# Plain fp32 products in place of three fp32r products of splits, in two transformer blocks with experts

## The chip, the cores and the metric

One core of a Trainium2 chip runs one program. Its engines work side by side, each through its own list of instructions in order, and wait for one another by semaphores: TensorE (PE; its weight loads are listed as PEld), VectorE (DVE), ScalarE (ACT), GpSimd (POOL) and SyncE (SP), whose queue issues nearly all transfers between HBM and the on-chip memory. The metric is the device time of one execution in microseconds, as the median of several runs. The profile shows one further execution.

## The reference

Two blocks run one after the other on 256 positions of width 1024, in fp32. The excerpt is cut to the products.

```python
# first block
u = rms_norm(h, attn_norm_g)
(dq, dk, dv, nq, kc, vc, ks, vs, kw, vw, ngate, mgate) = split(u @ w_in)
y_a = rms_norm(differential_attention(dq, dk, dv, lam), diff_subln_g) * (1 - lam_init)
y_b = g0 * o_c + g1 * o_s + g2 * o_w            # compressed, selected, windowed attention
h = h + (sigmoid(mg0) * (y_a @ w_branch_a) + sigmoid(mg1) * (y_b @ w_branch_b)) @ w_out
u = rms_norm(h, ffn_norm_g)
h = h + (silu(u @ w_gate) * (u @ w_up)) @ w_down
x = rms_norm(h, final_norm_g)
# second block
q, k, v, a, g = split(rms_norm(x, norm1_g) @ w_in_2)
conv = silu(layer_norm(depthwise_conv(a * sigmoid(g)) + conv_b))
x = x + concat(rms_norm(attn, attn_out_g), rms_norm(conv, conv_out_g)) @ w_out_2
h = rms_norm(x, norm2_g)
aff = softmax(h @ w_router)                      # each of 16 experts takes its 32 best positions
hid = silu(xs @ w_gate_2) * (xs @ w_up_2)        # 1024 -> 2048, per expert
out = rms_norm(x + scatter(gates * (hid @ w_down_2)), final_g)
```

## The kernel before

The 256 positions are two row blocks, t = 0 and t = 1, of 128. A wide linear layer is made in blocks of 512 output columns: `linear_steps` (L311) takes a slot with 2 MB of weights (eight pieces of 128 input rows by 512 columns), and the transposed activations `xt[t]`, and adds eight products per row block into one accumulator bank (tag `mm`, two banks).

Each of these products is made in three parts. `split` (L279) makes of a landed weight piece `wh`, a copy rounded to fp32r (ScalarE, L288), and `wl`, the rest (VectorE, L289). With a gain per row it does this in two halves through `put_hl` (L342; ScalarE L350, VectorE L351). Activations are split in the same way when they are copied out of the bank in which they were transposed. `mm3` (L297) then adds `xh·wh`, `xh·wl` and `xl·wh`. All matmuls of the first stage are recorded by the helper `MM` (L250), all transposes by `TP` (L255), so these lines stand for many places; the names of the tiles tell them apart: `mm` is a bank of a wide product, `dn` those of the feed forward's last layer, `tr` a bank for transposes, `sc` scores.

The order of TensorE's list is the order in which the code records it (`manual_schedule`). That order comes from `weave` (L234): several generators (compression, two flows of attention units, the mixer with the projections) yield the time after which they want to go on, on a clock `clock[0]` that `MM` moves on by an estimate of each product (512 columns: 0.213 us for fp32r, 0.853 for plain fp32). Work that waits for another engine is put in a list by `later(after, f)` and recorded by `flush` when the clock has passed.

The stages are: first block (nine blocks of `w_a`, one of `w_vg`, attention, `w_ab`, `w_o`); feed forward (`feed`, eleven blocks b of `w_gu` with 512 columns, 256 of gate and 256 of up, each followed by the layer down of block b - 1; `hid` is made by VectorE at L875 and transposed); second block (`w_b`, convolution, attention, `w_o2` in two halves with the activations `mixc` and `mixa`); router; 16 experts of 24 MB.

Expert weights are always plain fp32. `stream` hands out their slots by a list `turns` of twelve turns with 2 MB each; three turns are filled ahead, during the feed forward (`AH`). `ringd` (six half slots) takes the space of the split pieces after the first stage. The program on TensorE uses a slot's two 1 MB halves and so gives them back, and the next transfer of that turn is asked for on SyncE's queue.

Of the kernel before, what the change touches and what calls it, by code (L numbers as in the profile page):

```python
# [137 lines left out]
AH = [2, 7, 8]  # L138
ORDERS = [(0, 0, 0, 1, 0, 1, 1, 1), (0, 0, 0, 0, 1, 1, 1, 1), (0, 0, 1, 0, 0, 1, 1, 1), (0, 0, 0, 1, 1, 0, 1, 1), (0, 0, 1, 0, 1, 0, 1, 1), (0, 1, 0, 0, 1, 0, 1, 1)]
TURNS = [0, 4, 0, 0, 2, 0, 0, 0, 0, 0, 0, 0, 0, 0, 0, 0, 0, 0, 0, 0, 0, 0, 0, 0, 0, 0, 0, 0]  # L140

# [4 lines left out]
def _program(nc, tc, A, dbg=None):  # L146
# [9 lines left out]
    hres = es.enter_context(tc.tile_pool(name="hres", bufs=1, side="right"))  # L156
    t1 = ExitStack()
    sp = t1.enter_context(tc.tile_pool(name="sp", bufs=4))
    low = t1.enter_context(tc.tile_pool(name="low", bufs=4))
# [4 lines left out]
    low0 = [at1.enter_context(tc.tile_pool(name="low0", bufs=1))]  # L164
    spare = [at1.enter_context(tc.tile_pool(name="spare", bufs=1))]
# [40 lines left out]
    def slot_tile(pool=None):  # L206
        if pool is None:
            loads[0] += 1
            pool = ring0[0] if ring0 and loads[0] % 3 == 0 else ring
        return pool.tile([128, 4096], FT, tag="slot", name="slot")  # L210
# [38 lines left out]
    def MM(out, lhsT, rhs, start, stop):  # L249
        T.matmul(out, lhsT=lhsT, rhs=rhs, start=start, stop=stop)  # L250
        n, m = math.prod(rhs.shape[1:]), math.prod(lhsT.shape[1:])
        clock[0] += max(n, 128) * (1 if rhs.dtype == FR else 4) / 2400 * min(m, 128) / 128
# [23 lines left out]
    settings = iter(TURNS)  # L276
    splits, NX = [0], [1, 1]

    def split(src, n, gcol=None, fine=False):  # L279

        splits[0] += 1
        h = (spare[0] if spare and splits[0] % (4 + NX[0]) < NX[0] else sp).tile([128, n], FR, tag="wh", name="wh", padded_shape=[128, 1024])
        l = (low0[0] if low0 and splits[0] % (4 + NX[1]) < NX[1] else low).tile([128, n], FR, tag="wl", name="wl", padded_shape=[128, 1024])
        if fine:
            for c in (slice(0, n // 2), slice(n // 2, n)):
                put_hl(h[:, c], l[:, c], src[:, c])
        elif gcol is None:
            S.activation(h, src, AF.Copy)  # L288
            V.tensor_tensor(l, src, h.bitcast(FT), op=OP.subtract)  # L289
        else:  # L290
            w = n // 2
            for j in range(2):
                c = slice(j * w, (j + 1) * w)
                put_hl(h[:, c], l[:, c], src[:, c], col=gcol[:, j:j + 1])
        return h, l

    def mm3(out, xh, xl, wh, wl, start, stop):  # L297
        MM(out, xh, wh, start, False)
        MM(out, xh, wl, False, False)
        MM(out, xl, wh, False, stop)  # L300

# [9 lines left out]
    def linear_steps(slot, xt, evac, n=512, gcol=None, mid=None, ks=range(8), turn=None, fine=False):  # L311

        us = sorted({k // 2 for k in ks})
        turn = turn or ORDERS[next(settings)]
        hl = {j: split(slot[:, (j - us[0]) * 2 * n:(j - us[0] + 1) * 2 * n], 2 * n, None if gcol is None else gcol[:, 2 * j:2 * j + 2], fine and j < 2) for j in us}
        ps, at = [None] * 2, [0, 0]
        for t in turn:
# [5 lines left out]
            u = us[at[t]]  # L323
            at[t] += 1
            for k in (2 * u, 2 * u + 1):
                h, l = hl[u]
                c = slice((k % 2) * n, (k % 2 + 1) * n)
                mm3(ps[t][:, :n], xt[t][0][:, k], xt[t][1][:, k], h[:, c], l[:, c], k == ks[0], k == ks[-1])
            if at[t] == len(us):
                if mid is not None and t == 0:  # L330
                    mid()
                with tc.high_priority(1000):
                    evac(t, ps[t] if n == 512 else ps[t][:, :n])
# [3 lines left out]
    def linear(*args, **kw):  # L337
        for _ in linear_steps(*args, turn=(0, 0, 0, 0, 1, 1, 1, 1), **kw):
            pass
        flush()  # L340

    def put_hl(h, l, ps, scale=None, col=None):  # L342
        if scale is None and col is None:
            S.activation(h, ps, AF.Copy)
            V.tensor_tensor(l, ps, h.bitcast(FT), op=OP.subtract)
        elif col is None:
            S.activation(h, ps, AF.Copy, scale=scale)
            V.scalar_tensor_tensor(l, ps, scale, h.bitcast(FT), op0=OP.mult, op1=OP.subtract)
        else:
            S.activation(h, ps, AF.Identity, scale=col)  # L350
            V.scalar_tensor_tensor(l, ps, col, h.bitcast(FT), op0=OP.mult, op1=OP.subtract)  # L351

    def x_tiles(t):
        return [xtp.tile([128, 8, 128], FR, tag=f"xt{a}{t}", name="xt") for a in "hl"]

    def transposed(src, xt, c, scale=None, gain=None, tmp=None, high=False):

        ps = bank("tr")
        for j in range(4):
            TP(ps[:, j * 128:(j + 1) * 128], src[:, (4 * c + j) * 128:(4 * c + j + 1) * 128])  # L360
        h, l = (flat(z[:, 4 * c:4 * c + 4]) for z in xt)
        if gain is None:
            with tc.high_priority(1000 if high else 0):
                put_hl(h, l, ps, scale)
        else:
            gx = tmp()
            V.tensor_tensor(gx.rearrange("p (a b) -> p a b", a=4), ps.rearrange("p (a b) -> p a b", a=4),
                            gain[:, 4 * c:4 * c + 4, None].to_broadcast([128, 4, 128]), op=OP.mult)
            S.activation(h, gx, AF.Copy)
            V.tensor_tensor(l, gx, h.bitcast(FT), op=OP.subtract)  # L370
# [18 lines left out]
    def begin(t):  # L389
        for c in range(2):  # L390
            transposed(x0[:, t], xt[t], c, gain=attn_g, tmp=lambda: tp.tile([128, 512], FT, tag="ropeo", name="gx"))
# [225 lines left out]
    def nsa_unit(t, b, half):  # L617
# [34 lines left out]
        if todo["yb", t] == 0:  # L652
            ybT[t] = h_, l_ = [ap_.tile([128, 512], FR, tag=tag, name="ybT", padded_shape=[128, 528])
                               for tag in (("blk0", "blk1") if t == 0 else ("ybh1", "ybl1"))]
            put_hl(h_, l_, yb[t])
            mark(f"yb_done{t}", 3.3)

    def diff_unit(t, hp):
# [50 lines left out]
        if t == 0:  # L709
            todo["yah"] = ap_.tile([128, 2, 512], FR, tag="nqT", name="yah")  # L710
        yaT[t] = h_, l_ = todo["yah"][:, t], ap_.tile([128, 512], FR, tag=f"kT{t}", name="yal")
        put_hl(h_, l_, pt, col=sub8)
# [14 lines left out]

    mg = mgp.tile([128, 2, 4, 512], FT, tag="mg", name="mg")
# [8 lines left out]
    def mixer():  # L737
        W = lambda i: load(flat(A["w_a"][i]))
        yield from linear_steps(first, xt, ev_a, fine=True, turn=ORDERS[1][:1] + (begin1,) + ORDERS[1][1:])
# [4 lines left out]
        yield from linear_steps(W(4), xt, ev_dv)  # L744
        for n in range(4):
# [4 lines left out]
        for n in range(2):  # L750
            hl = [[split(wab[j][:, n * 2048 + u * 1024:n * 2048 + (u + 1) * 1024], 1024) for u in range(2)] for j in range(2)]
# [167 lines left out]
    steps = []  # L919
# [510 lines left out]
```

## Time and profile before

| | |
|---|---|
| median of 3 runs | 1444.31 us (1443.38 to 1444.76) |
| the profiled execution's own time | 1444.65 us |
| its span, first to last instruction | 1442.8 us |
| TensorE busy | 1110.6 us, 6451 matmuls |
| VectorE busy | 428.2 us |
| ScalarE busy | 322.7 us |
| transferred | 498.16 MB, mean 345 GB/s |
| granted clock of TensorE, mean | 0.897 of 2.4 GHz |

An engine's busy time is the time in which at least one of its instructions is recorded as running. Matmuls are pipelined, so one that lasts 0.39 us can be followed by the next after 0.23; what a product costs in a row of products is read from start to start. A line "x4" merges four instructions, from the first one's start to the last one's end. The chain of waits goes back from the last instruction, at each step to what released it.

### The profile page before, as it was taken

To read this page: it belongs to the slowest core of one execution; us is meant where nothing else is said; L and a number is where in the kernel's file an instruction comes from. 1 tells how busy PE (TensorE), PEld (TensorE's weight loads), DVE (VectorE), ACT (ScalarE), POOL (GpSimd) and SP (SyncE) were. 2 spreads that over 40 slices of the span, in tenths; PEclk is the share of its full clock that TensorE was granted. 3 is DMA by queue.
4 is the path that set the end of the run, shared out by engine and by line. 5 is a ranking of instruction groups with operands and counts; after the bars stand their busy time and mean duration, and the time that the engine had idled before them with its cause. 6 is when DMAs were issued, how large, how long until landed. Compare 5 with 4: busy or idle time off the path is not lost.

```text
span 1442.8 us, 15497 instructions
## 1 busy us (share of the span) xinstructions
PE 1110.6 (77%) x6451; PEld 557.9 (39%) x6451; DVE 428.2 (30%) x826; ACT 322.7 (22%) x583; POOL 33.5 (2%) x43
## 2 busy tenths in 40 slices
PE   7999999999999989766665665676666676666565
PEld 5777877888877773111211111121111121111112
DVE  6587675555562751101100100001000010010002
ACT  5466545555463630000000000000000000000001
POOL 1010000000000000000000000000000000000001
PEclk9999999999999999798998878788877897788889
DMA  8623247757546788999999999999999999999996
GB/s 313 260 92 124 100 186 284 278 219 269 176 168 191 291 339 366 427 429 431 428 429 429 429 431 427 429 431 429 429 426 429 431 427 430 428 430 430 427 429 290
DMA packets 52165, 498.16 MB, mean 345 GB/s; under 512 B 6016, under 2 KB 9088, under 8 KB 12160
## 3 DMA queue, kind: packets, MB, share of 16 engines
q1 hardware_dynamic: 52096, 497.18, 83.6%
q8 instruction: 51, 0.84, 0.2%
q14 instruction: 18, 0.15, 0.0%
HBM read 495.52 MB, written 1.64 MB: 345 GB/s over the span
## 4 chain that ended last, share of the span: by engine, by line
DMA 61%; PE 32%; DVE 4%; ACT 2%; issue 1%; SPq 0%; POOLq 0%; POOL 0%; ACTq 0%; DVEq 0%
DMA half<-in_e_d 21%; PE mm L250 21%; DMA half<-in_e_u 20%; DMA slot<-in_e_u 6%; DMA slot<-in_e_g 6%; PE dn L250 4%; PE sc L250 2%; DMA half<-in_e_g 2%; DMA slot<-in_e_dl 2%; DMA slot<-in_e_d 2%; PE tr L255 2%; PE mm L1305 2%; DVE wl L289 1%; DMA slot<-in_w_a 1%; DMA half<-in_e_dl 1%
## 5 line engine op out<-in xcount | busy, mean ns | idle before, releaser
L1305 PE MATMUL mm<-slot,xg 128*32 128x512 f32 x1536 | 240.1, 757 | 151.1 <-DMA slot<-in_e_u 96.3
L250 PE MATMUL mm<-wh,xt 128*128 128x512 f32 (+1 forms) x896 | 291.1, 395 | 2.8 <-DVE ropeb L446 1.8
L250 PEld LDWEIGHTS mm<-wh,xt 128*128 128x128 f32 x896 | 168.1, 189 | 41.6 <-issue 5.1
L1336 DVE TENSOR_TENSOR x<-acc,x 128x512 f32<-128x512 f32 x60 | 41.5, 691 | 462.1 <-PE acc L1334 462.1
L250 PE MATMUL mm<-wl,xt 128*128 128x512 f32 (+1 forms) x448 | 174.4, 389 | 0.7 <-DVE wl L289 0.4
L1329 PE MATMUL sc<-half,hT 128*32 128x512 f32 x720 | 122.1, 764 | 64.3 <-DMA half<-in_e_d 64.2
L1305 PEld LDWEIGHTS mm<-slot,xg 128*32 128x32 f32 x1536 | 47.7, 125 | 319.3 <-issue 119.9
L289 DVE TENSOR_TENSOR wl<-slot,wh 128x1024 fp32r<-128x1024 f32 (+1 forms) x104 | 124.6, 1211 | 73.5 <-ACT wh L288 72.8
L288 ACT ACTIVATE wh<-slot 128x1024 fp32r<-128x1024 f32 (+1 forms) x104 | 106.9, 1042 | 66.6 <-PE mm L250 49.8
L1312 DVE TENSOR_TENSOR sil<-sil,mm 128x512 f32<-128x512 f32 x16 | 11.0, 687 | 293.3 <-PE mm L1305 293.3
L1334 PE MATMUL acc<-eo,owT 128*128 128x512 f32 x120 | 78.1, 737 | 21.8 <-DVE x L1336 11.8
L250 PEld LDWEIGHTS mm<-wl,xt 128*128 128x128 f32 x448 | 84.6, 189 | 17.9 <-DVE wl L289 1.7
L1305 PE MATMUL mm<-half,xg 128*32 128x512 f32 x512 | 74.2, 666 | 20.2 <-DMA half<-in_e_u 11.0
L1350 ACT ACTIVATE eo<-sc 128x512 f32<-128x512 f32 x15 | 9.0, 597 | 357.2 <-PE sc L1329 357.2
L1329 PEld LDWEIGHTS sc<-half,hT 128*32 128x32 f32 x720 | 17.9, 123 | 163.2 <-DMA half<-in_e_d 142.7
L351 DVE SCALAR_TENSOR_TENSOR wl<-slot,pr,wh 128x512 fp32r<-128x512 f32 x88 | 62.8, 765 | 41.4 <-ACT wh L350 41.4
L1325 ACT ACTIVATE owT<-tr 128x256 f32<-128x256 f32 x16 | 6.1, 383 | 299.1 <-PE tr L1323 299.1
L350 ACT ACTIVATE wh<-slot,pr 128x512 fp32r<-128x512 f32 x88 | 58.1, 715 | 46.9 <-PE mm L250 31.2
L1329 PE MATMUL sc<-slot,hT 128*32 128x512 f32 x240 | 39.7, 791 | 26.6 <-DMA slot<-in_e_d 26.1
L1334 PEld LDWEIGHTS acc<-eo,owT 128*128 128x128 f32 x120 | 20.6, 216 | 89.5 <-DVE x L1336 33.5
L1311 ACT ACTIVATE sil<-mm 128x512 f32<-128x512 f32 x16 | 9.6, 597 | 192.4 <-PE mm L1305 192.4
L1305 PEld LDWEIGHTS mm<-half,xg 128*32 128x32 f32 x512 | 13.4, 119 | 72.2 <-DMA half<-in_e_u 41.3
(330 smaller groups left out, 972.4 us busy)
## 6 DMA issues: line engine op xcount, KB each, us to landing
slot<-in_e_g SPq DMA_DIRECT2D x48, 2048.0 KB, 24.4
slot<-in_e_u SPq DMA_DIRECT2D x48, 2048.0 KB, 29.2
half<-in_e_d SPq DMA_DIRECT2D x90, 1024.0 KB, 24.4
half<-in_e_g SPq DMA_DIRECT2D x32, 1024.0 KB, 29.2
half<-in_e_u SPq DMA_DIRECT2D x32, 1024.0 KB, 31.6
slot<-in_e_d SPq DMA_DIRECT2D x15, 2048.0 KB, 29.2
slot<-in_w_gu SPq DMA_DIRECT2D x11, 2048.0 KB, 8.1
slot<-in_w_a SPq DMA_DIRECT2D x7, 2048.0 KB, 8.7
```

Source lines behind the costliest of these rows:

```text
L250: T.matmul(out, lhsT=lhsT, rhs=rhs, start=start, stop=stop)
L255: T.transpose(out, src, ident if idn is None else idn)
L288: S.activation(h, src, AF.Copy)
L289: V.tensor_tensor(l, src, h.bitcast(FT), op=OP.subtract)
L350: S.activation(h, ps, AF.Identity, scale=col)
L351: V.scalar_tensor_tensor(l, ps, col, h.bitcast(FT), op0=OP.mult, op1=OP.subtract)
L1305: T.matmul(ps[32 * j:32 * j + 32], lhsT=xg[:, k, s0:s0 + 32], rhs=slot[kk][:, j * 512:(j + 1) * 512], start=k == 0, stop=k == 7)
L1311: S.activation(sil, gu[0], AF.Silu)
L1312: V.tensor_tensor(sil, sil, gu[1], op=OP.mult)
L1329: T.matmul(ps[32 * j:32 * j + 32, :c.stop - c.start], lhsT=hT2[:, q * 128 + 32 * j:q * 128 + 32 * j + 32], rhs=slot[n][:, j * 512 + c.star ...
L1334: T.matmul(ps, lhsT=owT[:, t * 128:(t + 1) * 128], rhs=eo, start=True, stop=True)
L1336: V.tensor_tensor(x[:, t, k], ps, x[:, t, k], op=OP.add)
```

## The change

All products named above are made once, in plain fp32, with the landed weights as moving operand. `split`, `mm3`, `put_hl` and the pools of the split pieces are gone; activations are copied out of the transpose bank once (`out_of`, in turn by ScalarE and VectorE, or VectorE with the gain). The gain of the feed forward's norm goes from the weights to the activations. In the space of the split pieces stands `ringl`, two full slots that serve for all loads and later for experts; `ringd` keeps two of six half slots. `linear_steps` has one default order, t = 0 and then t = 1, and in the feed forward a `flush` before each of the two. The clock counts every product at two columns per tick. The convolution's weights `w_cv` are loaded early in the first block.

```diff
-AH = [2, 7, 8]
-ORDERS = [(0, 0, 0, 1, 0, 1, 1, 1), ...]
+AH = [2, 5, 8]
...
+    ringl = es.enter_context(tc.tile_pool(name="ringl", bufs=2))
-    sp = t1.enter_context(tc.tile_pool(name="sp", bufs=4))
-    low = t1.enter_context(tc.tile_pool(name="low", bufs=4))
...
-        clock[0] += max(n, 128) * (1 if rhs.dtype == FR else 4) / 2400 * min(m, 128) / 128
+        clock[0] += max(n, 128) * 2 / 2400 * min(m, 128) / 128 * lhsT.shape[0] / 128
...
-    def mm3(out, xh, xl, wh, wl, start, stop):
-        MM(out, xh, wh, start, False)
-        MM(out, xh, wl, False, False)
-        MM(out, xl, wh, False, stop)
...
-    def linear_steps(slot, xt, evac, n=512, gcol=None, mid=None, ks=range(8), turn=None, fine=False):
+    def linear_steps(slot, xt, evac, n=512, ks=8, turn=(0, 0, 0, 0, 1, 1, 1, 1)):
...
-            for k in (2 * u, 2 * u + 1):
-                h, l = hl[u]
-                c = slice((k % 2) * n, (k % 2 + 1) * n)
-                mm3(ps[t][:, :n], xt[t][0][:, k], xt[t][1][:, k], h[:, c], l[:, c], k == ks[0], k == ks[-1])
+            for k in (at[t], at[t] + 1):
+                MM(ps[t][:, :n], xt[t][:, k], slot[:, k * n:(k + 1) * n], k == 0, k == ks - 1)
...
+    def out_of(dst, ps, scale=None):
+
+        turns_of[0] += 1
+        if turns_of[0] % 2:
+            S.activation(dst, ps, AF.Copy, scale=1.0 if scale is None else scale)
+        elif scale is None:
+            V.tensor_copy(dst, ps)
...
+        w_cv.append(load(flat(A["w_cv"]), pool=ringx))
...
-            yield from linear_steps(slot, xt, ev, gcol=pp("ffn_g"), turn=(flush, 0, 0, 0, 0, flush, 1, 1, 1, 1) if b == 0 else None)
+            yield from linear_steps(slot, xt, ev, turn=(flush, 0, 0, 0, 0, flush, 1, 1, 1, 1))
...
-    turns += [[ringc[0]], [ringc[1]], [ring], ringc[3:1:-1], [ring], [ringd[4], ringd[0]], [ringd[2], ringd[1]], [ringd[3], ringd[5]]]
+    turns += [[ringl], [ringc[0]], [ringc[1]], [ring], ringc[3:1:-1], [ring], ringd, [ringl]]
```

Two places show how TensorE's list moves. The first is a block of the feed forward. Before, the list of TensorE at the end of a block's 48 products (both row blocks, in three parts each):

```order
L250 MATMUL mm<-wh,xt 128x512 x2
L250 MATMUL mm<-wl,xt 128x512
L250 MATMUL mm<-wh,xt 128x512
L255 MATMUL tr<-fst,hid 128x128 x2
L250 MATMUL dn<-wh,hh 128x512
L250 MATMUL dn<-wl,hh 128x512
L250 MATMUL dn<-wh,hl 128x512
```

The same place in the changed kernel, one whole block (`slot` is the landed weights):

```order
L245 MATMUL mm<-slot,xt 128x512 x8
L250 MATMUL tr<-fst,hid 128x128 x2
L245 MATMUL mm<-slot,xt 128x512 x8
L245 MATMUL dn<-slot,hh 128x512 x8
L250 MATMUL tr<-fst,hid 128x128 x2
```

The transposes of t = 0 stood behind the products of both row blocks and now stand between them, right behind the products of t = 0 from which `hid` is made.

The second place is the end of the first attention: the difference units of t = 0 and t = 1 (`dkT`, `dqT` are their keys and queries, `a` the difference of the two softmaxes, `ya` its product with V, `yn` the normed result). Before, TensorE's list between the ya of t = 0 and the next step holds projections of the gate blocks:

```order
L250 MATMUL mm<-wl,xt 128x512
L250 MATMUL mm<-wh,xt 128x512
L250 MATMUL ya<-dv_1016,pt 128x128 x2
L250 MATMUL mm<-wh,xt 128x512
L250 MATMUL mm<-wl,xt 128x512
L250 MATMUL mm<-wh,xt 128x512 x2
```

The same place in the changed kernel, from the scores of the second unit of t = 0 on:

```order
L245 MATMUL sc<-dkT,dqT 128x128 x4
L250 MATMUL tr<-fst,a_963 128x128 x2
L245 MATMUL ya<-dv_580,pt 128x128 x2
L245 MATMUL sc<-dkT,dqT 128x256 x4
L250 MATMUL tr<-fst,a_1010 128x128 x2
L245 MATMUL ya<-dv_580,pt 128x128 x2
L250 MATMUL tr<-fst,a_1042 128x128 x4
L250 MATMUL tr<-fst,yn 128x128 x4
L245 MATMUL sc<-dkT,dqT 128x256 x4
L245 MATMUL mm<-slot,yaT 128x512 x4
```

The projections of the gates now all stand ahead of this place; between the steps of the units nothing wide is left.

## Rows read from the trace of the kernel before

**Rows 1.** The page's chain that ended last, shares of the span by engine.

```profile
DMA 61%; PE 32%; DVE 4%; ACT 2%; issue 1%; SPq 0%; POOLq 0%; POOL 0%; ACTq 0%; DVEq 0%
```

**Rows 2.** Windows: from:to, us, engines' busy us (instructions), clock, DMA share, GB/s.

```profile
0.00:212.00 212.00, 201.11 (x1176) 157.71 (x1177) 147.91 (x330) 117.81 (x227) 19.23 (x20) 1.00 0.49 183
212.00:376.00 164.00, 162.48 (x735) 133.27 (x734) 94.28 (x134) 88.30 (x134) 0.57 (x2) 1.00 0.64 244
376.00:545.50 169.50, 160.42 (x1016) 126.26 (x1018) 94.02 (x190) 84.09 (x150) 7.31 (x12) 0.97 0.64 238
```

**Rows 3.** A window among the experts, same columns (PE, PEld, DVE, ACT, POOL).

```profile
900.00:1100.00 200.00, 132.59 (x729) 29.82 (x722) 19.76 (x35) 5.33 (x10) 0.00 (x0) 0.80 1.01 429
```

**Rows 4.** Timeline at the seam: start, us, engine, line, operation, out<-in.

```profile
529.15 0.39 PE L250 MATMUL mm<-wh,mixa 128*128 128x512 f32 x1
...
529.58 1.28 SPq L805 DMA_DIRECT2D half<-in_e_d  x3
...
545.55 1.19 SPq L805 DMA_DIRECT2D half<-in_e_g  x2
```

**Rows 5.** The window just before the first freed slot.

```profile
540.00:545.00 5.00, 4.17 (x25) 2.93 (x28) 1.94 (x6) 0.52 (x1) 0.00 (x0) 0.69 0.43 179
```

**Rows 6.** TensorE's groups by form: tiles, count, busy us, mean ns, idle before.

```profile
L250 PE MATMUL mm<-wl,xt 128*128 128x512 f32 x432 | 169.7, 393 | 0.7 <-DVE wl L289 0.4 <-DVE sub L437 0.2
...
L250 PE MATMUL dn<-wl,hh 128*128 128x512 f32 x88 | 34.3, 390 | 0.0
...
L250 PE MATMUL mm<-wl,mixa 128*128 128x512 f32 x16 | 7.0, 434 | 0.0
...
L250 PE MATMUL mm<-wl,xt 128*128 128x280 f32 x16 | 4.7, 292 | 0.0
```

**Rows 7.** The chain of waits in the feed forward: start, us, what.

```profile
264.08 10.89 PE mm L250 x48
...
275.19 4.13 PE dn L250 x18
...
280.93 10.90 PE mm L250 x48
```

**Rows 8.** Plain products: timeline, and last the durations min/median/max of L1366.

```profile
550.29 8.79 PE L1305 MATMUL mm<-slot,xg 128*32 128x512 f32 x80
558.90 3.62 PE L1305 MATMUL mm<-half,xg 128*32 128x512 f32 x32
...
575.18 1.12 PE L1334 MATMUL acc<-eo,owT 128*128 128x512 f32 x2
576.24 1.06 PE L1305 MATMUL mm<-slot,xg 128*32 128x512 f32 x8
...
1420.23 1.13 PE L1366 MATMUL mm<-eo,owT 128*128 128x256 f32 x4 [0.50 <-ACT eo L1399]
...
L1366 PE MATMUL mm<-eo,owT x12: 275/379/483, 1420.2 to 1435.2; 128*128 128x256 f32 x8, 128*128 128x128 f32 x4
```

**Rows 9.** The page's group of VectorE's subtractions, busy us, mean ns.

```profile
L289 DVE TENSOR_TENSOR wl<-slot,wh 128x1024 fp32r<-128x1024 f32 (+1 forms) x104 | 124.6, 1211 | 73.5 <-ACT wh L288 72.8
```

**Rows 10.** Timeline of TensorE at the feed forward's first block; in brackets idle before.

```profile
222.64 0.39 PE L250 MATMUL mm<-wh,xt 128*128 128x512 f32 x1
224.17 0.44 PE L255 MATMUL tr<-fst,hid 128*128 128x128 f32 x2 [1.15 <-DVE hid L875]
```

**Rows 11.** Timeline of the difference units: scores, difference `a`, square, `yn`.

```profile
129.10 0.71 PE L250 MATMUL sc<-dkT,dqT 64*128 64x128 f32 x8
...
133.76 0.61 DVE L678 SCALAR_TENSOR_TENSOR a<-e,dsm 128x128 f32<-128x128 f32 x2
...
166.19 0.58 ACT L697 ACTIVATE yq<-ya 128x512 f32<-128x512 f32 x1
...
170.25 0.69 DVE L702 TENSOR_TENSOR yn<-ya,rsa 128x512 f32<-128x512 f32 x1
```

**Rows 12.** A window behind three short waits of the second attention.

```profile
515.00:520.00 5.00, 5.00 (x17) 3.96 (x16) 2.48 (x7) 0.63 (x2) 0.54 (x1) 0.70 1.02 429
```

## What the change should do to the time: the prediction

> **What bounds the kernel now.** I read the chain of waits first [rows 1]: 61% of the span hangs on landing transfers, 32% on TensorE, 4% on VectorE, 2% on ScalarE. Those shares mix two stages, so I cut the span. From 0 to 545.5 us [rows 2] TensorE shows 201.11, 162.48 and 160.42 us of work in stretches of 212, 164 and 169.5 us: 524.0 of 545.5, with transfers at 0.49 to 0.64 of their capacity. VectorE is at 336 us there, ScalarE at 290. So the first stage, both blocks and the feed forward, is bound by TensorE, and its idle time is only 21.5 us in all. The second stage, the experts, is bound by HBM: between 900 and 1100 us the engines of the transfers are full at 429 GB/s while TensorE idles a third of the time [rows 3].
>
> The seam decides how the first stage reaches the end. Expert weights run through 24 half slots of 1 MB. The last of these is asked for in a burst that begins at 529.58 us, and the next expert transfer after that burst starts at 545.55 us, when the first expert product has given a slot back [rows 4]. Between 540 and 545 us the transfer engines are only 0.43 busy [rows 5]: everything that fits has landed, and the stream waits for the first free slot. From there on it is saturated. So the end lies 1442.8 - 545.55 = 897.2 us after the first freed slot, and a delay of TensorE before it should move the end by the same amount.
>
> **The change, part by part.** *Products.* What goes: 600 groups of three fp32r products [rows 6]: 432 + 88 + 16 + 16 with "wl" as moving operand, and three more kinds of 16 like the mixa row (ybT, yah, mixc). Sixteen are 280 columns wide; by width that is 584 + 16 x 280/512 = 592.75 groups of 512. One fp32r product takes 10.89 us / 48 = 0.227 us from start to start, and a full period of the feed forward (72 products, 4 transposes) takes 280.93 - 264.08 = 16.85 us [rows 7]. A group costs 3 x 0.227 = 0.681 us.
>
> What comes in its place is one plain fp32 product, which the trace of before shows only in other shapes [rows 8]. Each plain product is recorded as two matmuls: the scatter's two per product. Eighty records of the experts' quarter-array products, four side by side, take 558.90 - 550.29 = 8.61 us, so 0.4305 us per set of four at 512 columns. The full-array product of 256 columns in the last expert gives four records (two products) in 1.13 us; the last lasts 0.379, the first 0.483 since it waits 0.104 for its own weights, so the steps are (1.13 - 0.379 - 0.104) / 3 = 0.216 us per record, with the loads of the later ones hidden. Twice the width makes at most 0.431. Both say 2 x 0.431 = 0.862 us per product of 512. The dear end is the scatter itself, 576.24 - 575.18 = 1.06 us, which stands alone between products of another shape. In the changed kernel the products stand in unbroken rows of 4 to 16, like the first two. I take 0.862; 0.861 is the low end, and 0.88 (a tenth of the way to 1.06) is where I end the range.
>
> So TensorE's own work grows: 592.75 x (0.862 - 0.681) = +107 us (+107 to +118).
>
> The Trainium skill has a rule against this change. "TensorE: Matmul & The Clock Gate", section "Part 3: Packing small matmuls — row/col tiling", says that a weight load runs under products in flight only if it is for another row group. All rows of the array are used here, so by that rule each of the two records would pay its load. The steps of 0.216 and 0.227 us in the trace contradict it, both with full-height weights. The sum by the rule stands among the rivals.
>
> *Splits.* The copies and subtractions that made high and low parts go: VectorE's 124.6 us at L289 alone [rows 9], and the copies that feed them on ScalarE. They lie beside TensorE's work; what their absence can return is at most the 21.5 us that TensorE idles. About 6 us of that is the start (transfers of x), 4 us the router, 1.2 us a wait that stays. I take -12 (0 to -21.5).
>
> *Feed forward, a new wait.* Before, both row blocks' products are interleaved and the transposes of `hid` follow all 48 of them. Now the order is eight products of t=0, at once its transposes, eight of t=1. Those transposes need Silu and the multiplication of what has just been accumulated. Before does this once, at the first block: last product at 222.64 us, transposes at 224.17, so 224.17 - 222.64 - 0.227 = 1.30 us in which TensorE has nothing [rows 10]; queued behind are the t=1 products. After has it in all 11 blocks, and once more for t=1 of the first: 12 places for one, +11 x 1.30 = +14 (12 to 18).
>
> *End of the first attention, a new wait.* The planner's clock now counts a wide product as 0.427 us where it takes 0.862, so fewer projections are laid between the attention's steps, and at the end of the last gate block they run out. Between the scores of the second difference unit of t=0 and the transposes of yn stand only some 2.3 us of small TensorE work. That chain took 5.3 us from scores to the finished difference, and 4.75 us from the square to yn [rows 11]; with 1.5 us for transposing, copying and multiplying by V it is 11.6 long, so 9.3 exposed. For t=1 the 4.75 us from square to yn are exposed once more: nothing stands between. Together +14. These chains ran beside the splits, and without them VectorE may do them in half the exposed time: +7; if the handovers between the engines add up at every step, +20.
>
> *Clock.* After three short waits the granted clock fell to 0.70 of 2.4 GHz between 515 and 520 us, and the stretch holds 17 matmuls instead of 22 [rows 12]: 5 x 0.227 = 1.1 us lost. In the longer waits above I count three such falls: +4 (0 to 10).
>
> *At nothing.* The convolution's weights are asked for before the second compression weight instead of in the feed forward: 2 MB at 429 GB/s is 5 us on SyncE's queue, and the first consumer of what stands behind it comes after 32 wide products, some 28 us; uncovered it would cost 5. Slots: the list of turns has 12 slots of 2 MB as before, but the last two (4 MB, 9.8 us) are now asked for only after the last mixa product; the same stretch before, from 529.15 [rows 4] to 545.55, is 16.4 us, so this is covered by 6.6. The feed forward's gain moves from the weights to the activations, one VectorE operation in place of another. The logits come in a bigger lump behind the last product: +1 (0 to 3).
>
> Sum: 107 + 14 + 14 + 4 + 1 - 12 = **+128 us**. On the profiled span, 1442.8 + 128 = 1571; its own time stood 1.85 us above its span and 0.34 above the median, so the median becomes **1572 us**, 8.9% slower.
>
> **Rivals.** *Faster: the plain product costs what the planner now says,* two columns per clock less, 0.427 us. Then -0.254 x 592.75 = -151, and with the waits (+33) and the splits (-12) the time is 1314 us. The sign turns where a product costs 0.681 - 21/592.75 = 0.645 us. For it speaks only that the number stands in the code; the records of 0.216 at 256 columns speak against it, since a product has two of them. Chance 0.04.
>
> *No change: the stream hides it.* If slots for another 128 us x 429 GB/s = 55 MB could be filled during the first stage, the end would stay at 1444. The list has 24 MB, and they are full at 542 us already [rows 5]. Chance 0.02.
>
> *Much slower: weight loads are not hidden* in a product's two records, as in the scatter row. Each product costs 0.862 + 2 x 0.104 = 1.07 us, the products +231 instead of +107, the time 1696 us. This is what the skill's rule above would make of it. Against it stand the two steady rows. Chance 0.03.
>
> *Slower beyond the range: the low clock lasts.* If the granted clock sat at half for the whole of both attention ends, some 35 us of work each, the time would be 1572 + 35 = 1607 or more. In before it is 1.00 in the first two stretches and 0.97 in the third [rows 2]. Chance 0.04.
>
> **How the numbers follow.** The forecast has 0.87, its rivals 0.04, 0.02, 0.03 and 0.04. The low end of the sum takes the cheap ends of three terms: 107 + 12 + 7 + 0 + 0 - 21.5 = +104, which is 1548; the high end 118 + 18 + 20 + 10 + 3 - 6 = +163, 1607. All ends at once is unlikely on either side, and no rival near them holds much chance, so the range is 1546 to 1600. A measurement of this kernel can tell about 0.2% from no change. Slower by more: 0.87 + 0.03 + 0.04 = 0.94; within: 0.02; faster: 0.04.
>
> **What would show it.** In the profile of the changed kernel: plain wide products in two records with 0.43 us between starts (0.53 would be the third rival, 0.215 the first); 24 products and their transposes per feed forward block in about 22.5 us instead of 16.85, with one wait of 1.3 on `hid` L875 in each; waits on `a` and `yn` at the end of the attention; no splits, VectorE's total down by some 200 us; the first expert slot free at about 674 us, transfers idle just before, and 897 us from there to the end. The forecast is wrong if that last distance is not constant, or if TensorE idles before the seam for more than some 60 us.

## The result, and the profile of the changed kernel

| | before | changed |
|---|---|---|
| median | 1443.85 us (1443.29 to 1444.76, 4 runs) | 1577.34 us (1573.45 to 1579.94, 4 runs) |
| ratio | | 1.0922, interval 1.0896 to 1.0947 |
| profiled execution, span | 1442.8 us | 1571.5 us |
| first expert slot free | 545.55 us [rows 4] | 676.95 us |
| from there to the end | 897.25 us | 894.55 us |

The change costs 133.5 us; the prediction had 128, and 1577 lies inside its range. The page's chain that ended last, shares of the span by engine, now reads (before: [rows 1]):

```profile
DMA 55%; PE 40%; DVE 2%; issue 2%; ACT 1%; SPq 0%; POOL 0%; POOLq 0%; ACTq 0%; DVEq 0%
```

TensorE's share has grown from 32 to 40%. The windows of the first block, the feed forward, the second block and router, and the experts (from:to, us, then busy us and instructions of PE, PEld, DVE, ACT and POOL, clock, DMA share, GB/s) show where:

```profile
0.00:265.20 265.20, 246.94 (x977) 125.52 (x978) 77.62 (x262) 57.78 (x158) 16.68 (x20) 0.97 0.43 163
265.20:514.60 249.40, 234.98 (x583) 103.98 (x582) 22.93 (x50) 20.54 (x42) 1.63 (x3) 1.00 0.44 166
514.60:677.00 162.40, 154.51 (x768) 86.76 (x770) 41.85 (x128) 41.61 (x97) 5.33 (x10) 0.94 0.57 212
677.00:1571.50 894.50, 571.17 (x3532) 144.57 (x3524) 91.99 (x174) 32.54 (x74) 6.42 (x10) 0.84 1.00 424
```

In the first three, which answer to [rows 2], TensorE has 636.4 us of work where it had 524, and idles 40.6 us instead of 21.5. VectorE does 142 us there instead of 336 (234.4 instead of 428.2 in the whole span, as foretold): the splits are gone, and nobody was waiting for most of them. The fourth stage is 2.7 us shorter than before (894.55 against 897.25). At the seam, the window before the first free slot (same columns) and SyncE's queue (start, us, what):

```profile
670.00:675.00 5.00, 3.25 (x18) 3.18 (x19) 2.25 (x9) 1.28 (x1) 0.00 (x0) 0.74 0.00 0
```

```profile
659.32 0.42 SPq L211 DMA_DIRECT2D slot<-in_e_d  x1
676.95 1.19 SPq L755 DMA_DIRECT2D half<-in_e_g  x2
```

Nothing moves in those 5 us: all slots are full, where [rows 5] still had the last ones landing, and the stream goes on at 676.95.

For the rest one needs the first stage by kind of time. From the trace's starts I take, for each matmul, the time to the next one's start. "Products" is the steady step (0.2265 us for an fp32r product of 512 columns, 0.429 for a plain record, narrower ones by width) times their number, "behind them" what a wide product's step has above that, "other" the steps of all smaller matmuls and transposes. The stages are cut at the first product of `w_gu` and of `w_b`; they end with the first expert product.

```
us              length   products  behind them  other
before  block 1  213.5     147.3      15.7       50.5
        ffn      188.7     179.3       5.5        3.9
        block 2  137.6      76.1       5.1       56.4
changed block 1  261.1     186.0       8.0       67.2
        ffn      249.4     226.5      16.5        6.3
        block 2  161.3      96.1       1.0       64.2
```

The products make +105.9 us of the 132 by which the stages grow, four fifths; the other two columns hide terms of both signs, in each of which the prediction has to be tried. TensorE's rows in one feed forward block, the counterpart of [rows 7] and [rows 10] (start, us, what, in brackets idle before and its releaser):

```profile
305.72 7.03 PE L245 MATMUL mm<-slot,xt 128*128 128x512 f32 x16
313.84 0.44 PE L250 MATMUL tr<-fst,hid 128*128 128x128 f32 x2 [1.08 <-DVE hid L819]
314.11 7.03 PE L245 MATMUL mm<-slot,xt 128*128 128x512 f32 x16
320.98 7.03 PE L245 MATMUL dn<-slot,hh 128*128 128x512 f32 x16
327.85 0.38 PE L250 MATMUL tr<-fst,hid 128*128 128x128 f32 x2
...
336.18 0.44 PE L250 MATMUL tr<-fst,hid 128*128 128x128 f32 x2 [1.09 <-DVE hid L819]
```

Sixteen records stand for eight products and take 7.03 us; the last record lasts 0.59, so the step is (7.03 - 0.59) / 15 = 0.429 us, and a product costs 0.858. From one `hid` wait to the next it is 336.18 - 313.84 = 22.34 us. The records' weight loads of 0.19 us lie inside; the first block of the feed forward waits longer, 2.42 us, with a table load on ScalarE ahead of it:

```profile
271.21 0.19 PEld L245 LDWEIGHTS mm<-slot,xt 128*128 128x128 f32 x1 [0.24 <-issue]
272.31 1.28 ACT L817 ACT_TABLE_LOAD   x1 [6.42 <-PE mm L245]
...
274.65 0.44 PE L250 MATMUL tr<-fst,hid 128*128 128x128 f32 x2 [2.42 <-DVE hid L819]
```

The end of the first attention reads:

```profile
183.22 0.68 PE L245 MATMUL ya<-dv,pt 128*128 128x128 f32 x4 [1.08 <-DVE pt L536]
...
190.34 1.21 PE L250 MATMUL tr<-fst,a 128*128 128x128 f32 x4 [2.97 <-DVE a L633]
193.02 1.09 PE L250 MATMUL tr<-fst,yn 128*128 128x128 f32 x4 [1.47 <-DVE yn L657]
...
196.05 4.63 PE L245 MATMUL mm<-slot,yaT 128*128 128x512 f32 x8
200.51 3.60 PE L245 MATMUL mm<-slot,ybT 128*128 128x512 f32 x8
...
210.83 0.66 PE L250 MATMUL tr<-fst,yn 128*128 128x128 f32 x4 [3.48 <-DVE yn L657]
```

The waits for `a` and `yn` are there. Behind them eight records take 4.63 us that take 3.60 a moment later: the low clock. The trace has the granted clock at the lower of its two levels (0.50 of 2.4 GHz, 1.2 GHz) in three long stretches of the first stage; the first begins inside the wait for `a`, the second just behind the last wait for `yn`, the third at a wait in the second attention (columns as above):

```profile
187.70:198.00 10.30, 6.18 (x19) 3.51 (x20) 5.24 (x18) 2.87 (x9) 1.03 (x1) 0.50 0.00 0
211.60:218.40 6.80, 6.13 (x10) 2.94 (x11) 0.00 (x0) 1.21 (x2) 0.76 (x1) 0.50 0.01 2
611.00:624.60 13.60, 12.68 (x56) 11.61 (x56) 8.32 (x18) 3.89 (x9) 1.58 (x3) 0.50 0.78 333
```

### The profile page after: what moved, and what is told of

Read it like the earlier page. It is cut to its first block, busy times and chain, and to the rows that moved or that the text cites. A ratio compares the mean times of both kernels' runs of the same rounds, so it can differ in the third digit from the quotient of the medians.

```text
span 1571.5 us, 13678 instructions
## 1 busy us (share of the span) xinstructions
PE 1207.6 (77%) x5851; PEld 460.8 (29%) x5851; DVE 234.4 (15%) x613; ACT 152.5 (10%) x370; POOL 30.1 (2%) x43
## 4 chain that ended last, share of the span: by engine, by line
DMA 55%; PE 40%; DVE 2%; issue 2%; ACT 1%; SPq 0%; POOL 0%; POOLq 0%; ACTq 0%; DVEq 0%
PE mm L245 27%; DMA slot<-in_e_u 18%; DMA slot<-in_e_g 12%; DMA half<-in_e_d 11%; DMA slot<-in_e_d 7%; PE dn L245 5%; PE sc L245 2%; DMA half<-in_e_g 2%; DMA half<-in_e_dl 2%; PE tr L250 2%; PE mm L1237 1%; DMA slot<-in_e_dl 1%; PE acc L245 1%; PE yb L245 1%; DMA slot<-in_x 0%
## 5 line engine op out<-in xcount | busy, mean ns | idle before, releaser
L245 PE MATMUL mm<-slot,xt 128*128 128x512 f32 (+1 forms) x896 | 391.7, 589 | 0.3 <-ACT xt L304 0.3
L1237 PE MATMUL mm<-slot,xg 128*32 128x512 f32 x1792 | 262.6, 714 | 155.8 <-DMA slot<-in_e_u 93.1
L245 PEld LDWEIGHTS mm<-slot,xt 128*128 128x128 f32 x896 | 165.9, 191 | 183.9 <-issue 181.4
L1261 PE MATMUL sc<-slot,hT 128*32 128x512 f32 x480 | 99.6, 976 | 103.0 <-DMA slot<-in_e_d 103.0
L1261 PE MATMUL sc<-half,hT 128*32 128x512 f32 x480 | 71.0, 680 | 23.5 <-DMA half<-in_e_d 23.4
L245 PE MATMUL dn<-slot,hh 128*128 128x512 f32 x176 | 77.5, 592 | 0.0
L1261 PEld LDWEIGHTS sc<-slot,hT 128*32 128x32 f32 x480 | 17.3, 148 | 168.0 <-DMA slot<-in_e_d 132.1
L245 PEld LDWEIGHTS dn<-slot,hh 128*128 128x128 f32 x176 | 33.3, 190 | 41.1 <-issue 41.1
L1237 PE MATMUL mm<-half,xg 128*32 128x512 f32 x256 | 35.4, 645 | 3.4 <-DMA half<-in_e_g 3.4
L525 ACT ACTIVATE e<-e,dmx 128x128 f32<-128x128 f32 (+1 forms) x48 | 21.2, 442 | 21.5 <-DVE dmx L523 21.4
```

What stands on the lines that cost most here:

```text
L525: S.activation(e, e, AF.Exp, bias=mx, scale=-1.0, accum_out=sm)
L1237: T.matmul(ps[32 * j:32 * j + 32], lhsT=xg[:, k, s0:s0 + 32], rhs=slot[kk][:, j * 512:(j + 1) * 512], start=k == 0, stop=k == 7)
L1261: T.matmul(ps[32 * j:32 * j + 32, :c.stop - c.start], lhsT=hT2[:, q * 128 + 32 * j:q * 128 + 32 * j + 32], rhs=slot[n][:, j * 512 + c.star ...
```

## Experiments

Medians of kernels on one chip are set against the kernel before on that chip (1443.1 to 1443.9 us). "First slot" is the time at which SyncE asks for the first expert piece after the seam, as above.

**The same kernel again.** 

> The changed kernel once more, with a second profile. Its four times lie 6.5 us apart, those of the kernel before 1.5. Theory: the difference is made in the first stage, where TensorE runs at the low granted clock behind the waits at the two attention ends (0.79 between 180 and 220 us in the first profile): median 1573 to 1580, and in the new profile the first expert slot comes free within 7 us of 676.95 with 894 to 895 us from there to the end. Rival: the difference is made among the experts; then the slot comes free within 1 us of 676.95 and the distance to the end changes instead.

Measured: 1575.06 us (1573.65 to 1576.87), ratio 1.0905 (1.0889 to 1.0921). In the second profile the first slot is free at 679.77, 2.8 us later, and the end follows 895.13 us behind (894.55). So the difference between these two profiles arises in the first stage. Which wait made it is not settled by two profiles.

**No middle flush.**

```diff
-            yield from linear_steps(slot, xt, ev, turn=(flush, 0, 0, 0, 0, flush, 1, 1, 1, 1))
+            yield from linear_steps(slot, xt, ev, turn=(flush, 0, 0, 0, 0, flush, 1, 1, 1, 1) if b == 0 else (0, 0, 0, 0, 1, 1, 1, 1))
```

> The changed kernel with the feed forward's second flush left only in its first block, so that from the second block on the products of t=1 stand between those of t=0 and the transposes of its hid. Theory: ten waits of 1.25 us, all that TensorE lacks in those blocks, go and nothing takes their place: -12.5 us, the period of a block falls from 22.34 to 21.1 us, the first slot is free at 664 us and the median is 1564 or 1565. Rival: the transposes wait for hid or a bank wherever they stand, or the loads of the next block become the bound: within 3 us of the changed kernel.

Measured: 1562.14 us (1557.41 to 1563.18), 12.9 below the changed kernel on the same chip; first slot at 664.86. TensorE's rows of one block:

```profile
305.33 13.90 PE L245 MATMUL mm<-slot,xt 128*128 128x512 f32 x32
319.07 0.38 PE L250 MATMUL tr<-fst,hid 128*128 128x128 f32 x2
319.28 7.03 PE L245 MATMUL dn<-slot,hh 128*128 128x512 f32 x16
326.15 0.38 PE L250 MATMUL tr<-fst,hid 128*128 128x128 f32 x2
326.37 13.90 PE L245 MATMUL mm<-slot,xt 128*128 128x512 f32 x32
```

No brackets are left, and the period is 326.37 - 305.33 = 21.04 us. The ten waits were worth 12.9 us, and nothing took their place.

**The clock at true prices.**

```diff
-        clock[0] += max(n, 128) * 2 / 2400 * min(m, 128) / 128 * lhsT.shape[0] / 128
+        clock[0] += max(n, 128) * 4 / 2400 * min(m, 128) / 128 * lhsT.shape[0] / 128
```

> The changed kernel with the planner's clock counting a product at four columns per tick and not two, which is the 0.43 us per record of the trace. Theory: the waits at the end of the first attention (a, yn and pt, 16.5 us above the steady steps between 181 and 213 us, and about 6 us of low clock behind them) stand there because the projections ran out too early; with true prices projections remain for them: -12 to -18 us, median 1559 to 1565, TensorE's idle time between 180 and 220 us down from 11.6 to under 5. Rival: the chain of the last difference units is longer than what the projections can cover, and the waits only move to another place in the block: within 5 us of the changed kernel.

The edit raises the price from two ticks of 2.4 GHz per column to four, 0.853 us for a product of 512 columns; what is called "columns per tick" above means ticks per column.

Measured: 1541.85 us (1541.54 to 1542.37), 33.2 below the changed kernel: about twice what was expected. TensorE in stretches of the two attention ends, first the changed kernel, then this one (columns as above):

```profile
180.00:190.00 10.00, 5.19 (x37) 3.21 (x36) 7.14 (x33) 5.07 (x19) 0.00 (x0) 0.89 0.04 18
190.00:200.00 10.00, 8.19 (x23) 4.40 (x24) 4.57 (x18) 2.76 (x9) 1.03 (x1) 0.60 0.00 0
200.00:210.00 10.00, 6.60 (x30) 3.93 (x28) 3.59 (x7) 1.19 (x2) 0.96 (x1) 1.00 0.34 105
210.00:220.00 10.00, 8.39 (x18) 4.14 (x19) 1.21 (x2) 1.28 (x2) 2.36 (x2) 0.66 0.01 2
...
610.00:620.00 10.00, 8.70 (x39) 8.22 (x40) 6.38 (x13) 3.17 (x7) 1.78 (x4) 0.55 1.00 429
```

```profile
180.00:190.00 10.00, 10.00 (x25) 4.47 (x24) 0.00 (x0) 2.86 (x4) 2.35 (x1) 1.00 0.47 141
190.00:200.00 10.00, 10.00 (x27) 4.45 (x26) 2.75 (x4) 0.00 (x0) 0.00 (x0) 1.00 0.39 162
...
610.00:620.00 10.00, 10.00 (x32) 4.93 (x32) 3.77 (x9) 1.57 (x5) 0.54 (x1) 1.00 1.01 429
```

The first block is 242.2 us long instead of 261.1 (-18.9) and the second 149.7 instead of 161.3 (-11.6). The -18.9 are what was expected and a little more: 11.6 us of idle time between 180 and 220 us are gone, and some 6 of low clock (an estimate: half of the 6.18 and 6.13 us of work that ran at 0.50). The -11.6 were in nobody's account. The second attention has the same defect: the changed kernel lays no wide product between 598 and 628 us, and then

```profile
611.23 3.65 PE L245 MATMUL acc<-v,pt 128*128 128x64 f32 x16 [3.29 <-DVE z L993]
...
616.51 4.00 PE L245 MATMUL acc<-v,pt 128*128 128x64 f32 x16
...
632.05 1.89 PE L245 MATMUL acc<-v,pt 128*128 128x64 f32 x16
```

The wait is only 3.3 us, but from 611.0 to 624.6 us the clock is at 0.50, and the same sixteen small products take 3.65 and 4.00 us instead of 1.89. With true prices products of `mixc` stand between them, and this one runs them at 1.89 each. Over the second block its idle time is 4.0 us less (3.9 instead of 7.9), and half of the 12.68 us of work at the low clock is 6.3: together 10.3 of the 11.6.

**Both edits.**

```diff
-        clock[0] += max(n, 128) * 2 / 2400 * ...
+        clock[0] += max(n, 128) * 4 / 2400 * ...
...
-            yield from linear_steps(slot, xt, ev, turn=(flush, 0, 0, 0, 0, flush, 1, 1, 1, 1))
+            yield from linear_steps(slot, xt, ev, turn=(flush, 0, 0, 0, 0, flush, 1, 1, 1, 1) if b == 0 else (0, 0, 0, 0, 1, 1, 1, 1))
```

> Both edits together, no middle flush after the first block of the feed forward and the clock at four columns per tick. Theory: they touch different stages, so the gains add: -25 to -31 us, median 1546 to 1552, still 7% above the kernel before, because the products themselves cost 105 us more. Rival: what one gains the other has already, or transfers become late: no more than the better of the two alone.

Measured: 1528.12 us (1526.75 to 1529.38), ratio 1.0579 (1.0563 to 1.0595), 46.9 below the changed kernel; the two gains make 46.1 one by one. They add; the expected range of 25 to 31 was too small only because that of the planner's price was. What is left, 84.2 us above the kernel before, is the price of the products less a gain of some 22.

**Plain products in the order of before, with all splits.**

```diff
-        MM(out, xh, wh, start, False)
-        MM(out, xh, wl, False, False)
-        MM(out, xl, wh, False, stop)
+        T.matmul(out, lhsT=xh.bitcast(FT), rhs=wh.bitcast(FT), start=start, stop=stop)
+        clock[0] += 3 * max(wh.shape[-1], 128) / 2400
```

> The kernel before in its own order and with all its splits, but each group of three is one plain fp32 product of the two high parts (the products with low parts are left out; the clock still counts three). Theory: a product costs 0.858 instead of 0.681 us, 592.75 times, +105 us; the 15 to 20 us in which TensorE waited for splits in the kernel before go too, since splits have a quarter more time for each product: median 1530 to 1537. Rival: those waits go only where the splits themselves are gone: median 1547 to 1551.

Measured: 1535.93 us (1534.02 to 1539.81), +92.5; first slot at 636.25. The time is where the theory had it: 105.9 us for the products, less 13 that come back although VectorE still makes every split (433.2 us busy in all). Where they come back shows when the n-th product starts, against the kernel before, with the dearer products (0.858 - 3 x 0.2265 = 0.1785 us per 512 columns) taken off:

```
n           48     224     488     600 (end of stage)
this       -6.1    -9.2    -8.9   -14.3 us
both edits -6.6    -9.9   -12.0   -18.2 us
```

Some two fifths of the gain are there after the first 48 products, 55 us into the kernel. Windows and a timeline of the kernel before show why (columns as above):

```profile
20.00:25.00 5.00, 4.15 (x19) 3.17 (x18) 3.21 (x9) 4.96 (x8) 0.53 (x1) 1.00 1.01 406
25.00:30.00 5.00, 4.03 (x19) 2.87 (x17) 5.00 (x7) 1.70 (x3) 1.52 (x2) 1.00 0.51 169
```

```profile
24.31 4.31 DVE L289 TENSOR_TENSOR wl<-slot,wh 128x1024 fp32r<-128x1024 f32 x3
...
29.07 0.73 DVE L446 SCALAR_TENSOR_TENSOR ropeb<-mm,rstd,sin 128x192 f32<-128x192 f32 x2
...
29.94 0.47 PE L250 MATMUL mm<-wh,xt 128*128 128x512 f32 x1 [0.97 <-DVE ropeb L446]
```

First ScalarE, then VectorE is full, mostly with splits of weights that land all at once, and TensorE lacks nearly a fifth of its work. What it waits for in the second window is not a split but `ropeb`, which empties the bank of a wide product and stands behind 4.31 us of subtractions. With dearer products the same splits and `ropeb` are in time: no such wait is left. This run also leaves TensorE no low part to read; in the kernel before the waits that end with one (`wl`, `hl`) come to 1.0 us of idle time, so that alone is little, but steps which it stretches without idle time are not told apart. What frees the other eight us, behind the 48th product, no run singles out. In the kernel with both edits, which has no splits at all, only some 4 us more come back.

**The same without the weights' splits.**

```diff
         (in split)
-        S.activation(h, src, AF.Copy)
-        V.tensor_tensor(l, src, h.bitcast(FT), op=OP.subtract)
+        h = l = src
```

> As the kernel with one plain product and all splits, but the landed weights are the moving operand and their splits are gone (left out: the products with low parts, and the gain of the feed forward's norm). Theory: the splits were already hidden behind plain products, so within 4 us of that kernel. Rival: the splits cost TensorE time in waits and handovers: 12 to 20 us less than that kernel, about 1531.

Measured: 1579.74 us (1578.04 to 1584.34), 43.8 more. The theory and its rival both fall. TensorE's waits in the first stage (engine, line, what for; us in total, times, longest):

```profile
PE mm L285 <- DMA slot<-in_w_o: 17.5, 2, 10.0
PE mm L285 <- DMA slot<-in_w_gu: 8.0, 9, 1.0
...
PE mm L285 <- DMA slot<-in_w_b: 4.8, 1, 4.8
PE sc L250 <- DMA slot<-in_w: 4.4, 1, 4.4
```

Weights land late. A split is also a copy: once it is made the landing slot is free, and the next 2 MB can be asked for while TensorE still multiplies. Without splits a slot is held until its last product. That this is the cause is argued here from the waits; the next run tries it.

**Three landing slots in the changed kernel.**

```diff
-            pools = [ring, ring, ringl, ringl] + ring0
+            pools = [ring, ring] + ring0
```

> The changed kernel, but the loads of the first stage use only the three full slots that the kernel before had for them, and the two slots in the space of the split pieces serve for the experts alone. Theory: with plain products a slot is held until its last product, where the splits gave it back a copy earlier; with three slots the loads come late as they did in the order of the kernel before without weight splits, where TensorE waited 36 us in all for landing weights: +25 to +40 us, median 1600 to 1615. Rival: in the changed order three slots suffice: within 5 us of the changed kernel's 1575 to 1577.

Measured: 1615.21 us (1614.01 to 1618.45), 38 to 40 above the two medians of the changed kernel; first slot at 717.58. Again the waits of the first stage:

```profile
PE tr L250 <- DVE hid L819: 14.4, 12, 2.4
PE mm L245 <- DMA slot<-in_w_o: 9.8, 1, 9.8
PE mm L245 <- DMA slot<-in_w_gu: 9.5, 9, 1.5
...
PE mm L245 <- DMA slot<-in_w_a: 5.1, 1, 5.1
...
PE mm L245 <- DMA slot<-in_w_b: 4.7, 1, 4.7
```

The changed kernel itself has no wait for `w_o`, `w_gu`, `w_a` or `w_b` in that list. So the two slots in the freed space, `ringl`, are what keeps the loads at nothing.

**No subtractions for the weights, three fp32r products.**

```diff
         (in split)
-        V.tensor_tensor(l, src, h.bitcast(FT), op=OP.subtract)
+        l = h
```

> The kernel before without VectorE's subtractions for the weights: the low part of a weight is left out and the high part stands in its place, so three fp32r products of the same cost remain. Theory: of the 21.5 us in which TensorE idles in the first stage, some 5 to 12 are waits for these subtractions and for the copies behind them: median 1432 to 1439. Rival: ScalarE's copies or the loads are late instead, or nothing was late: 1442 to 1446.

Measured: 1436.91 us (1436.68 to 1439.23), ratio 0.9955 (0.9939 to 0.9971): -6.5 us for 180 us of VectorE's work (428.2 us busy in all before, 247.8 here). After 48 products the kernel is ahead by 5.6 us, so nearly all of it is the start: at the old price of a product TensorE is now busy for the whole of both windows shown above (20 to 30 us). Less work for VectorE does there what dearer products did.

**Two fp32r products.**

```diff
         MM(out, xh, wh, start, False)
-        MM(out, xh, wl, False, False)
-        MM(out, xl, wh, False, stop)
+        MM(out, xh, wl, False, stop)
```

> The kernel before with two of the three fp32r products (the one with the low part of the activation is left out), splits as before. Theory: TensorE binds the first stage and the experts' stage has a fixed length behind the first free slot, so the time falls by the work removed, 592.75 x 0.227 = 135 us, less what VectorE, which has 336 us of work in the remaining 411, now makes late: 1309 to 1335, with 895 to 899 us from the first free slot to the end. Rival: the splits or the loads bind at once, or the end does not follow the seam: over 1360.

Measured: 1383.30 us (1380.24 to 1386.36, 2 runs), -60 of the 135 us removed. The theory's 1309 to 1335 is missed, and the time lies in its rival's range. The end follows the first slot (486.89) by 897.7 us as foreseen, but in the first stage TensorE is no longer the bound. The feed forward's window:

```profile
200.00:361.00 161.00, 143.45 (x586) 103.44 (x585) 105.30 (x150) 94.26 (x150) 0.55 (x1) 0.98 0.72 280
```

No engine is full here. TensorE idles 17.5 us and steps slower than it could; its waits are spread over roundings, subtractions, `yn` and `hid`.

**One fp32r product.**

```diff
-        MM(out, xh, wh, start, False)
-        MM(out, xh, wl, False, False)
-        MM(out, xl, wh, False, stop)
+        MM(out, xh, wh, start, stop)
+        clock[0] += max(wh.shape[-1], 128) / 2400
...
         (in put_hl, in turn)
+        S.activation(h, ps, ...)
+        V.tensor_copy(h, ps)
```

> The kernel before with one fp32r product of the rounded parts in place of three (all low parts left out, and with them every subtraction; the roundings go in turn to ScalarE and VectorE; the clock counts two products, as in the kernel with two). TensorE's work in the first stage falls by 592.75 x 0.454 = 269 us, which would give 1175, near the 1161 us that 498 MB take at 429 GB/s. Theory: the kernel with two products gave back only 60 of 135 us because splits came late behind VectorE; here their work is less than half, so far more comes back: median 1240 to 1310. Rival: it was the order's short distances between dependent steps that held it, and they stand: 1350 to 1385.

Measured: 1301.08 us (1299.56 to 1302.77), ratio 0.9017 (0.9003 to 0.9030), faster than both kernels by leaving all low parts out. First slot at 403.01, end 895.9 us later. TensorE's longest waits are for the roundings:

```profile
PE mm L250 <- ACT wh L340: 25.4, 9, 4.3
PE mm L250 <- DVE wh L344: 13.5, 4, 4.6
```

The run takes away splits and products together, so it does not tell how much of the 82 us against two products is due to either.

## Why the prediction was right, step by step

**The seam.** Right, and the firmest part. In twelve profiles, with the first slot free between 403 and 718 us, the end came 894.6 to 897.7 us later. A microsecond of TensorE before the seam is a microsecond of the total, in both directions.

**The products.** Predicted 0.862 us each and +107; measured 0.858 and +105.9. The price read from narrower and from quarter-array rows [rows 8] was good to half a percent, and the rivals at 0.43 and at 1.07 are out. The Trainium skill's rule ("TensorE: Matmul & The Clock Gate", "Part 3: Packing small matmuls — row/col tiling"), by which each record here would pay its weight load, does not agree with this trace: the steps are 0.429 us with full-height loads of 0.19 in them. Another page of the Trainium skill, "FP8 and Floating Point Precision", section "TensorE Precision Notes", says that true fp32 takes four passes through the array; 0.858 us against 0.227 for one fp32r product is 3.8, which agrees.

**The feed forward's wait.** Predicted +14; removing it in ten blocks gave 12.9. The wait in the first block, which the prediction left as it was (1.15 us [rows 10]), grew to 2.42: ScalarE loads a table for 1.28 us between the product and the first Silu. With true prices that wait is 1.3 us shorter again.

**The end of the first attention, and the clock.** At the place that it names the term was near: +14 for the waits and +4 for the clock, where the trace has 11.6 us of idle time and some 6 of low clock, and true prices gave the first block 18.9 back. As a whole it was too small, 18 against 33.2, in two ways. The clock was costed as three falls of 1.1 us (put at 4), from a row at 0.70 for 5 us [rows 12]; in fact the low level lasted for 10.3, 6.8 and 13.6 us, and half of the 25.0 us of work in these stretches, some 12 us by this estimate, was lost, more than the term's own upper end of 10. The rival of a lasting low clock has a slip besides: 35 us of work in each of two ends at half the clock would add 70 and not 35. And the planner's wrong price was followed to one place only. It is one number that orders all of both blocks, and in the second attention it cost 11.6 us more. One link is told the wrong way round: with a wide product at half its price the planner lays more of them between two steps of the attention, not fewer. 161 of the 600 stand ahead of the first difference scores in the changed kernel, 100 with true prices; that is why they have run out at the end, which the prediction had right.

**The splits' absence.** Predicted -12 (0 to -21.5); the both-edits kernel shows -19.1 in the first stage (632.35 - 545.55 - 105.9). That is a remainder and holds whatever else the change moved. The reason given is not needed for most of it: 15.2 of it come in the kernel with one plain product and all splits (636.25 - 545.55 - 105.9). At the start the runs point to VectorE's queue, which either dearer products or fewer subtractions relieve; for the rest the cause stays open.

**At nothing.** The loads do cost nothing in the changed kernel, but the prediction did not name what covers them, the two slots of `ringl`: without these, +38 to +40 us. The cover that it named, the distance to the first consumer of what stands behind `w_cv`, was not tried by itself. The last two expert turns, asked for until 659.32 us, were full at the seam, as costed.

**Sum.** 105.9 for the products, 12.9 for the flush, 33.2 for the planner's price, -19.1 and another -2.6 because the experts' stage is shorter by that in these kernels: 130.3 us, where the second measurement of the changed kernel stands 131.2 above the kernel before. As the -19.1 is a remainder, this tests only that the two edits add. The logits' +1 was not singled out. The mechanism was right in its main parts, the seam, the products and the flush; that the total came within 6 us is partly luck, since the planner's term was 15 too small and the gain that was laid to the splits some 10 too small, and the two errors have opposite signs.

## What to carry over

When a tensor product gets another price, follow the number by which the program was ordered through every stage that it orders, and count the clock that is lost behind each wait as well as the wait. A copy that seems to be pure cost may be what frees a landing buffer early: before taking it out, ask how many slots are held until when. The gain that comes with a change need not come from the part that was removed; undo that part alone before crediting it.

## What was not expected of the hardware

A short wait can cost more in clock than in idle time: 3.3 us of waiting between 608 and 611 us, behind 10 us of small products, were followed by 13.6 us at the lower level (0.50), in which sixteen small products took 4.00 us instead of 1.89. Plain fp32 records are very even: of 1097 steps from one wide record to the next in the changed kernel's first stage, 90% lie between 0.429 and 0.432 us. Why the changed kernel's first four times spread over 6.5 us, its second four over 3.2, and those of the two kernels with true prices over 1 and 3, is open; that the latter lack the waits behind which the clock falls is an argument, not shown.
